# A hybrid decoder layer: ten of 22 row pairs of each down matrix in seven block products instead of eight, and a tile shared with the memory's keys and values

## The chip, the cores and the metric

The kernel runs on one core of one Trainium2 chip, as one program in one launch. The metric is the device time of one execution in microseconds (us), lower is better. In the text TensorE is PE, VectorE is DVE, ScalarE is ACT, GpSimd is POOL, and SyncE is SP, which issues every DMA.

## What is computed

One layer on 256 tokens of width 1024: a SwiGLU feed-forward with layer norm, three token mixers that share an input projection (window attention, block attention, and cross attention into 256 memory tokens), gates, an output projection with layer norm, and a second SwiGLU with layer norm. The change touches the two feed-forwards (hidden width 2816) and the place of the memory's keys and values.

```python
def swiglu(x, w_gate, w_up, w_down):
    return (jax.nn.silu(x @ w_gate) * (x @ w_up)) @ w_down

x = layer_norm(DN_ALPHA * x + 0.5 * swiglu(x, ffn1_w_gate, ffn1_w_up, ffn1_w_down), ln1_g, ln1_b)
...
kv = mem @ w_mem_kv + b_mem_kv
...
x = layer_norm(DN_ALPHA * x + 0.5 * swiglu(x, ffn2_w_gate, ffn2_w_up, ffn2_w_down), ln3_g, ln3_b)
```

## The kernel before

**Weights.** All weights lie in 1 MB chunks of 128 x 2048. A chunk is loaded into one of three raw buffers (tile `raw`), then split into a rounded part and a remainder: ACT casts `whi` (line 136), DVE subtracts and writes `wlo` (line 137). `whi` and `wlo` have four buffers each; a chunk's buffers come free when PE has made its last matmul with them. An fp32 product is three matmuls (`product`, lines 209 to 211): high by high, low by high, high by low. Near the end of the first feed-forward, from the last four chunks of its down matrix to the second feed-forward's chunk 3, a chunk is split in four quarters of 512 columns each.

**Feed-forward.** For each of 11 chunks of 256 hidden features, `ffn` makes the gate and up products, the activation, and the hidden tile `h`, split into `hh` and `hl`. Then `down` goes through the 11 chunks of the down matrix in the order of `DOWN[n]`; this text calls the place of a chunk in it its position, 0 to 10. An ordinary chunk makes eight products (2 rows of 128 features x 2 halves of the tokens x 2 halves of the columns), 24 matmuls of 512 columns. At the positions in `SEVEN` a chunk is taken as a 2 x 2 block product with seven multiplications (Strassen-Winograd), 21 matmuls. For this DVE makes four sums of `h` (lines 482 to 485), which are split like `h` into one of the tiles `pairs`, two chunks to a tile, and `seven_parts` (line 183) makes three sums of the weights into the one tile `t` (lines 188 to 190) and then splits three quarters of the raw chunk and `t` itself, so that it takes two `whi` and two `wlo` buffers.

```python
DOWN = {1: list(range(NC)), 2: [2, 0, 4, 1, 6, 3, 8, 5, 7, 9, 10]}
SEVEN = (0, 2, 4, 6)
KEEP = 3
```

The last three positions (`KEEP`) are held: their products are made for the first half of the tokens, then for the second, so that the norm of one half can begin while PE works on the other. Before them, after position 7, `settle` and `more` (lines 408 to 424) add the seven-product banks of PSUM into the residual `x_sb`: an ACT copy `e` of bank 1, then nine DVE instructions.

**After the first down stage.** `load_mem` (line 543) loads the 256 memory tokens transposed (tile `mem`, in the place of `t`) and splits them into `memT`, two tiles: one ACT cast and one DVE subtraction of 128 x 2048. PE goes on with the memory's keys (chunk `mk`, line 577), transposes of the normed tokens, the memory's values (`mv`), then the chunks `qa0`, `qa1` and `v0` of the input projection. Keys and values lie in `km` and `vm`, lines 560 and 561.

**The order.** SP's instructions run in the order in which the code writes them: `load_to` and `load_mem` in turn, so the load of the memory tokens is queued behind that of `qa0`'s chunk. The instructions of PE, ACT and DVE are put in order by a scheduler when the program is built; on the chip each engine runs its own in that order and waits on semaphores.

Of the kernel before, what the change touches and what calls it, by code (L numbers as in the profile page):

```python
# [11 lines left out]
F32R = mybir.dt.float32r  # L12
# [5 lines left out]
P = 128  # L18
S = 256
# [4 lines left out]
NC = NF // 2  # L24
# [5 lines left out]
SLOPES = [2.0 ** (-8.0 * (i + 1) / 6) for i in range(6)]  # L30


DOWN = {1: list(range(NC)), 2: [2, 0, 4, 1, 6, 3, 8, 5, 7, 9, 10]}
SEVEN = (0, 2, 4, 6)
KEEP = 3


# [3 lines left out]
def plan():  # L41
# [5 lines left out]
    def cols(name, c0):  # L47
        return lambda d: tiles(d[name][0][:, c0 : c0 + 256], 256)

    def rows(name, r0):  # L50
        return lambda d: tiles(d[name][0][r0 : r0 + 256], D)
# [11 lines left out]
    def half(name, i):  # L63

        return lambda d: tiles(d[name][0][i * 512 : (i + 1) * 512, :512], 512)
# [3 lines left out]
    def ffn(n):  # L69
        for c in range(NC):  # L70
            for k, w in (("g", "gate"), ("u", "up")):
                lead = n == 2 and c < 2
                chunks.append(((k, n, c), f"lead{k}" if lead and c == 0 else None,
                               half(f"ffn{n}_w_{w}", c) if lead else cols(f"ffn{n}_w_{w}", c * 256)))
        for i, c in enumerate(DOWN[n]):
            chunks.append((("d", n, c), "seven" if i in SEVEN else None, rows(f"ffn{n}_w_down", c * 256)))

# [43 lines left out]
def hybrid_layer(ctx: ExitStack, tc: tile.TileContext, a: dict, out: bass.AP):  # L121
# [4 lines left out]
    const = ctx.enter_context(tc.tile_pool(name="const", bufs=1))  # L126
    raws = ctx.enter_context(tc.tile_pool(name="raws", bufs=3))
    parts = ctx.enter_context(tc.tile_pool(name="parts", bufs=4))
    acts = ctx.enter_context(tc.tile_pool(name="acts", bufs=1))
# [4 lines left out]
    def split(src, hi, lo):  # L134

        nc.scalar.copy(hi, src)  # L136
        return nc.vector.tensor_sub(lo, src, hi.bitcast(F32))  # L137
# [58 lines left out]
    def weights(key, ahead=2):  # L196
        i = index[key]
        load_to(i + 6)
        part_to(i + ahead)
        return part_of.pop(i)  # L200
# [17 lines left out]
    def tok(t):  # L218
        return slice(t * P, (t + 1) * P)
# [5 lines left out]
    def feature_tile_2(ps, w, col, x, ks=range(KD), parts_=(0, 1)):  # L225

        for part in parts_:
            for k in ks:
                wk = w[part][:, k * 256 + col : k * 256 + col + P]
                if part == 0:  # L230
                    nc.tensor.matmul(ps, wk, x.both[:, k], start=k == 0, stop=False)  # L231
                else:
                    nc.tensor.matmul(ps[:, S:], wk, x[0][:, k], start=False, stop=k == KD - 1)  # L233

    def added(dst, ps):

        b = work.tile([P, 512], F32, name="b", tag="w")[:, :S]
        nc.scalar.copy(b, ps[:, S:])  # L238
        nc.vector.tensor_add(dst, ps[:, :S], b)
# [91 lines left out]
    def halves(name, tags):  # L331

        t = [acts.tile([P, n, S], F32R, name=f"{name}{i}", tag=tags[i]) for i, n in enumerate((12, 10))]
        return lambda k, n=1: t[0][:, k : k + n, :] if k < 12 else t[1][:, k - 12 : k - 12 + n, :]
# [37 lines left out]
    def down(n, lhs, sums, resid, after, between=None, ends=HALVES):  # L372


        order = DOWN[n]
        bank = {b: acc.tile([P, 512], F32, name="ps") for b in (1, 6, 5, 7, 2, 3, "x", 4)}
        n7, n8 = len(SEVEN), len(order) - KEEP - len(SEVEN)
        left = {b: n7 for b in (1, 5, 6, 7)} | {b: n7 + 2 * (n8 + KEEP) for b in (2, 3, 4)} | {"x": 2 * n8}
# [13 lines left out]
        for i, c in enumerate(order):  # L392
            w = weights(("d", n, c), 1 if i >= len(order) - KEEP else 2)
            if i in SEVEN:
                (s1, s2, s3, s4), (b, t) = sums[c], w
# [44 lines left out]
    def gated(g, u):  # L440

        s = work.tile([P, 512], F32, name="s", tag="w")
        nc.scalar.activation(s, g, AF.Silu)
        h = work.tile([P, 512], F32, name="h", tag="w")
        nc.vector.scalar_tensor_tensor(h, u, 0.5, s, op0=ALU.mult, op1=ALU.mult)
        return h

    def ffn(n, x, resid, after, start=0, hooks={}, h=None, between=None, ends=HALVES):
        hh, hl = h or (halves("hh", ("A1", "A2")), halves("hl", ("B1", "B2")))
        sevens = [DOWN[n][i] for i in SEVEN]  # L450
        pairs = [acts.tile([P, 2, 2, 4, P], F32R, name=f"s{i}", tag=t) for i, t in enumerate(("C", "E"))]
        sums = {}
        for c in range(start, NC):
            if c in hooks:
                hooks[c](hh, hl)
            gu = []

            ps = {}
            for ks in FIRST if n == 1 and c == 0 else [range(KD)]:
                for key in ("g", "u"):  # L460
                    if ks.start == 0:
                        ps[key] = weights((key, n, c)), [mm.tile([P, 512], F32, name="ps") for _ in range(2)]
                    if len(ks) < KD:
                        for part in range(2):
                            for j in range(2):
                                feature_tile_2(ps[key][1][j], ps[key][0], j * P, x, ks, (part,))
                    else:
                        for j in range(2):
                            feature_tile_2(ps[key][1][j], ps[key][0], j * P, x)
                    if ks.stop == KD:  # L470
                        v = work.tile([P, 512], F32, name=key, tag="w")
                        for j in range(2):
                            added(v[:, j * S : (j + 1) * S], ps[key][1][j])
                        gu.append(v)
            y = gated(*gu)
            split(y.rearrange("p (j s) -> p j s", s=S), hh(2 * c, 2), hl(2 * c, 2))
            if c in sevens:

                a11, a21, a12, a22 = (y[:, tok(i)] for i in range(4))
                s = work.tile([P, 512], F32, name="s", tag="w")  # L480
                s1, s2, s3, s4 = (s[:, tok(i)] for i in range(4))
                nc.vector.tensor_add(s1, a21, a22)
                nc.vector.tensor_sub(s3, a11, a21)
                nc.vector.tensor_sub(s2, s1, a11)
                nc.vector.tensor_sub(s4, a12, s2)
                i = sevens.index(c)
                both = pairs[i // 2][:, i % 2]
                split(s.rearrange("p (i c) -> p i c", c=P), both[:, 0], both[:, 1])
                sums[c] = [(both[:, 0, m], both[:, 1, m]) for m in range(4)]
        down(n, lambda k, t: (hh(k)[:, 0, tok(t)], hl(k)[:, 0, tok(t)]), sums, resid, after, between, ends)  # L490
# [59 lines left out]
    def norm1(t, pss):  # L550
        if "x1" not in late:
            late["x1"] = const.tile([P, 2, D], F32, name="x1_sb", tag="X1")
        norm_into(x_sb, late["x1"], scale=1.0)(t, pss)

    ffn(1, x0T, x_sb, norm1, hooks={4: hook_1, 7: hook_2}, between=load_mem)
    memT, x1 = late["memT"], late["x1"]
    x1T = tokens_of("x1T")


    km = tuple(const.tile([P, 2, S], F32R, name=f"km{i}") for i in range(2))  # L560
    vm = tuple(const.tile([P, 2, 256], F32R, name=f"vm{i}") for i in range(2))

    def biased(ps, bc, hi, lo):

# [265 lines left out]
    def finish(t, pss):  # L830
        def put(t, s, r):
            return r, lambda: nc.sync.dma_start(out=out[0, tok(t), s], in_=r)
        normalize(t, pss, x2, put, scale=1.0)

    ffn(2, x2T, x2, finish, start=2, hooks={3: hook_lead}, h=h2, ends=((0, 512), (512, 768), (768, D)))
    for key in ("g", "u"):
        queue_behind(x2T_last, lows[index[key, 2, 2]])
# [30 lines left out]
```

## Time and profile before

| | us |
|---|---|
| median of 3 runs | 573.85 |
| lowest and highest | 573.81, 574.36 |
| the profiled execution | 573.77 |
| its span, first to last instruction | 572.0 |
| PE busy in the span | 561.8 (98%) |
| DVE busy | 452.7 (79%) |
| ACT busy | 326.2 (57%) |

The profile is of one execution. The span leaves out 1.77 us of the profiled execution's time that lies around it. A busy PE is an engine with an instruction under way; where two matmuls follow each other at the pace of their width, it does not wait. Idle time of DVE or ACT costs nothing by itself.

### The profile page before, as it was taken

To read this page: it belongs to the slowest core of one execution; us is meant where nothing else is said; L and a number is where in the kernel's file an instruction comes from. 1 tells how busy PE (TensorE), PEld (TensorE's weight loads), DVE (VectorE), ACT (ScalarE), POOL (GpSimd) and SP (SyncE) were. 2 spreads that over 40 slices of the span, in tenths; PEclk is the share of its full clock that TensorE was granted. 3 is DMA by queue.
4 is the path that set the end of the run, shared out by engine and by line. 5 is a ranking of instruction groups with operands and counts; after the bars stand their busy time and mean duration, and the time that the engine had idled before them with its cause. 6 is when DMAs were issued, how large, how long until landed. Compare 5 with 4: busy or idle time off the path is not lost.

```text
span 572.0 us, 8735 instructions
## 1 busy us (share of the span) xinstructions
PE 561.8 (98%) x3378; PEld 498.3 (87%) x3378; DVE 452.7 (79%) x707; ACT 326.2 (57%) x569; POOL 23.6 (4%) x37
## 2 busy tenths in 40 slices
PE   8999999999999999999999999999999999999994
PEld 7888888888888998999999999888888888888883
DVE  5898667878888998699787677997666777889686
ACT  6786555546653652965974765543565656464600
POOL 2000000000000000000002022210000000000001
PEclk9999999999999999999999999999999999999998
DMA  8886756535655275084163655546555645444502
GB/s 277 311 296 260 282 172 269 178 119 213 227 222 221 80 298 211 7 347 164 29 226 116 220 170 200 183 156 248 222 182 187 201 167 210 158 149 170 199 0 73
DMA packets 18025, 108.98 MB, mean 191 GB/s; under 512 B 2112, under 2 KB 2368, under 8 KB 5696
## 3 DMA queue, kind: packets, MB, share of 16 engines
q1 hardware_dynamic: 17984, 108.43, 52.5%
q8 instruction: 26, 0.43, 0.3%
q14 instruction: 15, 0.12, 0.1%
HBM read 107.37 MB, written 1.05 MB: 190 GB/s over the span
## 4 chain that ended last, share of the span: by engine, by line
PE 92%; ACT 3%; DVE 2%; DMA 1%; issue 0%; SPq 0%; POOLq 0%; DVEq 0%
PE ps L231 29%; PE ps L210 15%; PE ps L209 15%; PE ps L211 15%; PE ps L233 15%; ACT whi L136 1%; DMA xT<-in_xT_dram 1%; ACT sc_b L664 1%; PE ps L688 1%; PE ps L277 1%; DVE sc_b L648 1%; DVE m L653 0%; PE ps L641 0%; ACT gates L724 0%; DVE r L523 0%
## 5 line engine op out<-in xcount | busy, mean ns | idle before, releaser
L137 DVE TENSOR_TENSOR wlo<-raw,whi 128x512 fp32r<-128x512 f32 (+3 forms) x242 | 230.2, 983 | 64.1 <-ACT whi L136 57.7
L136 ACT CAST whi<-raw 128x512 fp32r<-128x512 f32 (+3 forms) x242 | 194.0, 845 | 96.8 <-PE ps L211 39.7
L231 PE MATMUL ps<-x0T,whi 128*128 128x512 f32 x352 | 89.5, 393 | 0.9 <-DVE x0T L137 0.5
L231 PEld LDWEIGHTS ps<-x0T,whi 128*128 128x128 f32 x352 | 62.8, 189 | 12.2 <-ACT whi L136 1.3
L231 PE MATMUL ps<-x2T,whi 128*128 128x512 f32 x288 | 72.2, 392 | 0.0
L231 PEld LDWEIGHTS ps<-x2T,whi 128*128 128x128 f32 x288 | 51.8, 189 | 9.3
L209 PE MATMUL ps<-x1T,whi 128*128 128x256 f32 x192 | 55.2, 287 | 0.3 <-ACT sc_m L664 0.3
L211 PE MATMUL ps<-x1T,wlo 128*128 128x256 f32 x192 | 54.3, 283 | 0.0
L210 PE MATMUL ps<-x1T,whi 128*128 128x256 f32 x192 | 54.3, 283 | 0.0
L210 PE MATMUL ps<-wlo,hh 128*128 128x512 f32 (+1 forms) x142 | 54.0, 380 | 0.0
L209 PE MATMUL ps<-whi,hh 128*128 128x512 f32 (+1 forms) x142 | 54.0, 380 | 0.0
L211 PE MATMUL ps<-whi,hl 128*128 128x512 f32 (+1 forms) x142 | 54.0, 380 | 0.0
L233 PEld LDWEIGHTS ps<-x0T,wlo 128*128 128x128 f32 x352 | 48.8, 190 | 4.1 <-DVE wlo L137 0.2
L233 PE MATMUL ps<-x0T,wlo 128*128 128x256 f32 x352 | 50.0, 282 | 0.0
L238 ACT COPY b<-ps 128x256 f32<-128x256 f32 x92 | 33.4, 368 | 25.8 <-PE ps L233 24.2
L233 PEld LDWEIGHTS ps<-x2T,wlo 128*128 128x128 f32 x288 | 39.3, 190 | 2.8
L233 PE MATMUL ps<-x2T,wlo 128*128 128x256 f32 x288 | 40.2, 282 | 0.0
L209 PEld LDWEIGHTS ps<-x1T,whi 128*128 128x128 f32 x192 | 36.8, 191 | 0.8 <-ACT sc_m L664 0.5
L210 PEld LDWEIGHTS ps<-x1T,whi 128*128 128x128 f32 x192 | 36.8, 192 | 0.0
L211 PEld LDWEIGHTS ps<-x1T,wlo 128*128 128x128 f32 x192 | 36.8, 191 | 0.0
L209 PEld LDWEIGHTS ps<-whi,hh 128*128 128x128 f32 x142 | 26.7, 188 | 5.1
L210 PEld LDWEIGHTS ps<-wlo,hh 128*128 128x128 f32 x142 | 26.7, 188 | 5.1
(195 smaller groups left out, 892.9 us busy)
## 6 DMA issues: line engine op xcount, KB each, us to landing
raw<-in_w_dram SPq DMA_DIRECT2D x92, 1024.0 KB, 4.8
raw<-in_w_dram SPq DMA_DIRECT2D x16, 256.0 KB, 5.3
ln<-in_ln_dram SPq DMA_DIRECT2D x3, 1024.0 KB, 7.0
xT<-in_xT_dram SPq DMA_DIRECT2D x4, 256.0 KB, 6.3
x_sb<-in_x_dram SPq DMA_DIRECT2D x1, 1024.0 KB, 7.0
mem<-in_memT_dram SPq DMA_DIRECT2D x1, 1024.0 KB, 8.4
out_dram<-r SPq DMA_DIRECT2D x3, 256.0 KB, 2.0
brow<-in_by_column_dram SPq DMA_DIRECT2D x1, 387.0 KB, 8.4
```

The costliest lines, as they stand in the source:

```text
L136: nc.scalar.copy(hi, src)
L137: return nc.vector.tensor_sub(lo, src, hi.bitcast(F32))
L209: nc.tensor.matmul(ps, lh, rh, start=first and i == 0, stop=False)
L210: nc.tensor.matmul(ps, lh, rl, start=False, stop=False)
L211: nc.tensor.matmul(ps, ll, rh, start=False, stop=last and i == n - 1)
L231: nc.tensor.matmul(ps, wk, x.both[:, k], start=k == 0, stop=False)
L233: nc.tensor.matmul(ps[:, S:], wk, x[0][:, k], start=False, stop=k == KD - 1)
L238: nc.scalar.copy(b, ps[:, S:])
L277: nc.tensor.transpose(ps[:, j * P : (j + 1) * P], src[:, k * P : (k + 1) * P], ident)
L648: nc.vector.scalar_tensor_tensor(sc[:, len(raw), :], dist[nm], -SLOPES[h] / SCALE, ps[:, :w], op0=ALU.mult, op1=ALU.add)
L664: nc.scalar.activation(sc[:, e, c0:c1], raw[e][:, c0:c1], AF.Exp, bias=negm[:, e, t : t + 1], scale=SCALE, accum_out=ssum[:, e, t : t + 1])
L688: nc.tensor.transpose(pt[:, s * n + j * P : s * n + (j + 1) * P], sc[:, 2 * i + s, c : c + P], ident)
```

## The change

`SEVEN` gets a fifth position and is now 0, 1, 3, 5 and 7, for both feed-forwards; `DOWN[2]` is put in another order, so that the chunks computed first come first. The block sums of the fifth chunk need a third tile. It is a tile of the constant pool under the name `KV`, and the memory's keys and values, which were four tiles of their own, are now slices of one tile `kv` of the same size in the same place: the sums of the first feed-forward lie there before the keys and values are written, those of the second after they were last read.

```diff
-DOWN = {1: list(range(NC)), 2: [2, 0, 4, 1, 6, 3, 8, 5, 7, 9, 10]}
-SEVEN = (0, 2, 4, 6)
+DOWN = {1: list(range(NC)), 2: [2, 3, 0, 4, 1, 6, 5, 8, 7, 9, 10]}
+SEVEN = (0, 1, 3, 5, 7)
...
-        pairs = [acts.tile([P, 2, 2, 4, P], F32R, name=f"s{i}", tag=t) for i, t in enumerate(("C", "E"))]
+        pairs = [pool.tile([P, 2, 2, 4, P], F32R, name=f"s{i}", tag=t)
+                 for i, (pool, t) in enumerate(((acts, "C"), (acts, "E"), (const, "KV")))]
...
-    km = tuple(const.tile([P, 2, S], F32R, name=f"km{i}") for i in range(2))
-    vm = tuple(const.tile([P, 2, 256], F32R, name=f"vm{i}") for i in range(2))
+    kv = const.tile([P, 4, 2, S], F32R, name="kv", tag="KV")
+    km, vm = (tuple(kv[:, 2 * j + i] for i in range(2)) for j in range(2))
```

Over both feed-forwards PE has 30 matmuls of 512 columns fewer with `hh` and `hl` and 24 more with the sums, six fewer in all. SP's and POOL's instructions stand as before. The scheduler put those of DVE, ACT and PE in another order around the down stages. (Line numbers from `ffn` on are one higher in the changed kernel.)

DVE in the middle of the first down stage, one position of eight products and the next of seven. Before, from the remainder of position 4's `t` (1477) over positions 5 (1512) and 6 (1542 its chunk, 1545 its sums `t`) to the remainder of position 6's `t` (1544):

```order
L137 TENSOR_TENSOR wlo_1477<-t_1478,whi_1476 128x2048
L188 TENSOR_TENSOR t_1545<-raw_1405 128x1024
L137 TENSOR_TENSOR wlo_1512<-raw_1344,whi_1511 128x2048
L189 TENSOR_TENSOR t_1545<-raw_1405,t_1545 128x512
L190 TENSOR_TENSOR t_1545<-raw_1405,t_1545 128x512
L137 TENSOR_TENSOR wlo_1542<-raw_1405,whi_1541 128x512
L137 TENSOR_TENSOR wlo_1542<-raw_1405,whi_1541 128x1024
L137 TENSOR_TENSOR wlo_1544<-t_1545,whi_1543 128x2048
```

In the changed kernel, from the remainder of position 3's `t` (1455) over positions 4 (1490) and 5 (1520, 1523) to the remainder of position 5's `t` (1522):

```order
L137 TENSOR_TENSOR wlo_1455<-t_1456,whi_1454 128x2048
L137 TENSOR_TENSOR wlo_1490<-raw_1295,whi_1489 128x2048
L188 TENSOR_TENSOR t_1523<-raw_1352 128x1024
L137 TENSOR_TENSOR wlo_1520<-raw_1352,whi_1519 128x512
L189 TENSOR_TENSOR t_1523<-raw_1352,t_1523 128x512
L137 TENSOR_TENSOR wlo_1520<-raw_1352,whi_1519 128x1024
L190 TENSOR_TENSOR t_1523<-raw_1352,t_1523 128x512
L137 TENSOR_TENSOR wlo_1522<-t_1523,whi_1521 128x2048
```

The three sums into `t` stood ahead of the chunk's own remainders; now they alternate with them, and the last sum (line 190) stands directly ahead of the remainder of `t`.

ACT at the end of the first down stage, from the copy `e` of bank 1: `whi` of position 10, of `mk`, of `mv`, `qa0` and `qa1`, in quarters. Before (1707 is position 10, 1719 `mk`, 1844 `mv`, 1924 `qa0`, 2012 `qa1`):

```order
L418 COPY e_1681<-ps_1397 128x512
L136 CAST whi_1707<-raw_1539 128x512 x4
L136 CAST whi_1719<-raw_1576 128x512 x4
L136 CAST whi_1844<-raw_1612 128x512 x2
L136 CAST memT0_1699<-mem_1697 128x2048
L136 CAST whi_1844<-raw_1612 128x512 x2
L136 CAST whi_1924<-raw_1645 128x512 x4
```

In the changed kernel (1716 is position 10, 1728 `mk`, 1850 `mv`, 1930 `qa0`, 2018 `qa1`):

```order
L418 COPY e_1690<-ps_1415 128x512
L136 CAST whi_1716<-raw_1554 128x512 x4
L136 CAST whi_1728<-raw_1584 128x512 x4
L136 CAST whi_1850<-raw_1621 128x512 x4
L136 CAST whi_1930<-raw_1657 128x512 x3
L136 CAST memT0_1708<-mem_1706 128x2048
L136 CAST whi_1930<-raw_1657 128x512
```

The cast of the memory tokens stood behind two quarters of `mv`; now it stands behind all four of `mv` and three of `qa0`.

PE among the held positions, first half of the tokens (1401 and 1402 are the two banks of its columns; 1647 and 1707 positions 9 and 10). Before:

```order
L210 MATMUL ps_1401<-wlo_1648,hh1_192 128x512
L211 MATMUL ps_1401<-whi_1647,hl1_194 128x512
L209 MATMUL ps_1401<-whi_1707,hh1_192 128x512
L210 MATMUL ps_1401<-wlo_1708,hh1_192 128x512
L211 MATMUL ps_1401<-whi_1707,hl1_194 128x512
```

In the changed kernel (1419 and 1420 the two banks, 1422 a bank of the second half; 1623, 1659 and 1716 positions 8, 9 and 10):

```order
L210 MATMUL ps_1420<-wlo_1717,hh1_192 128x512
L211 MATMUL ps_1420<-whi_1716,hl1_194 128x512
L210 MATMUL ps_1419<-wlo_1717,hh1_192 128x512
L211 MATMUL ps_1419<-whi_1716,hl1_194 128x512
L209 MATMUL ps_1420<-whi_1716,hh1_192 128x512
L209 MATMUL ps_1422<-whi_1623,hh1_192 128x512
L210 MATMUL ps_1422<-wlo_1624,hh1_192 128x512
L210 MATMUL ps_1420<-wlo_1717,hh1_192 128x512
```

Before, position 10's products of one bank followed each other; now its products with the later quarters of `wlo_1717` are put off behind products of the other bank and of the second half of the tokens.

## Rows read from the trace of the kernel before

**Rows 1.** Top of the page, parts 1 and 2.
```profile
span 572.0 us, 8735 instructions
...
PE 561.8 (98%) x3378; PEld 498.3 (87%) x3378; DVE 452.7 (79%) x707; ACT 326.2 (57%) x569; POOL 23.6 (4%) x37
...
PEclk9999999999999999999999999999999999999998
```

**Rows 2.** Waits of the weight loads: total us, times, longest.
```profile
PEld ps L209 <- ACT sc_m L664: 0.5, 1, 0.5
PEld ps L210 <- DVE memT L137: 0.2, 1, 0.2
PEld ps L210 <- DVE p L137: 0.5, 2, 0.3
```

**Rows 3.** TensorE timeline: start us, duration us, instruction.
```profile
129.84 0.40 PE L209 MATMUL ps<-whi,hh 128*128 128x512 f32 x1
...
140.07 0.39 PE L209 MATMUL ps<-whi,hh 128*128 128x512 f32 x1
...
170.67 0.39 PE L209 MATMUL ps<-whi,hh 128*128 128x512 f32 x1
...
186.99 0.40 PE L209 MATMUL ps<-memT,whi 128*128 128x256 f32 x2
187.42 0.39 PE L210 MATMUL ps<-memT,whi 128*128 128x256 f32 x1
...
506.49 0.40 PE L209 MATMUL ps<-whi,hh 128*128 128x512 f32 x1
...
563.78 0.28 PE L211 MATMUL ps<-whi,hl 128*128 128x256 f32 x1
```

**Rows 4.** VectorE timeline, the two down stages; columns as above.
```profile
144.30 2.29 DVE L137 TENSOR_TENSOR wlo<-t,whi 128x2048 fp32r<-128x2048 f32 x1 [0.94 <-ACT whi L136]
146.63 1.23 DVE L188 TENSOR_TENSOR t<-raw 128x1024 f32<-128x1024 f32 x1
147.77 2.28 DVE L137 TENSOR_TENSOR wlo<-raw,whi 128x2048 fp32r<-128x2048 f32 x1
149.97 0.68 DVE L189 TENSOR_TENSOR t<-raw,t 128x512 f32<-128x512 f32 x1
150.69 0.69 DVE L190 TENSOR_TENSOR t<-raw,t 128x512 f32<-128x512 f32 x1
...
156.71 2.49 DVE L137 TENSOR_TENSOR wlo<-raw,whi 128x512 fp32r<-128x512 f32 x4
...
166.19 0.68 DVE L414 SCALAR_TENSOR_TENSOR x_sb<-x_sb,e 128x512 f32<-128x512 f32 x1
166.79 0.68 DVE L410 TENSOR_TENSOR y<-e,ps 128x512 f32<-128x512 f32 x1
...
173.40 3.09 DVE L137 TENSOR_TENSOR wlo<-raw,whi 128x512 fp32r<-128x512 f32 x5
...
520.95 2.29 DVE L137 TENSOR_TENSOR wlo<-t,whi 128x2048 fp32r<-128x2048 f32 x1 [0.94 <-ACT whi L136]
```

**Rows 5.** Busy us by engine in 160 to 180, clock.
```profile
160.00:180.00 20.00, 20.00 (x90) 16.55 (x89) 17.34 (x29) 9.09 (x17) 0.00 (x0) 1.00 0.67 248
```

**Rows 6.** ScalarE timeline, end of the first down stage.
```profile
129.09 1.57 ACT L136 CAST whi<-raw 128x512 fp32r<-128x512 f32 x2 [1.41 <-PE ps L231]
...
181.75 1.14 ACT L136 CAST whi<-raw 128x512 fp32r<-128x512 f32 x2 [8.70 <-PE ps L211]
182.95 1.91 ACT L136 CAST memT<-mem 128x2048 fp32r<-128x2048 f32 x1
```

**Rows 7.** SyncE timeline, issue of the memory load.
```profile
174.48 0.43 SPq L546 DMA_DIRECT2D mem<-in_memT_dram  x1
```

**Rows 8.** Memory tile's own view, time from issue to landing.
```profile
DMA to landing us min/median/max: 8.4/8.4/8.4
```

**Rows 9.** Engines and granted clock of the last stretch, columns as rows 5.
```profile
568.00:570.00 2.00, 0.00 (x0) 0.00 (x0) 0.50 (x2) 0.00 (x0) 0.00 (x0) 0.53 0.74 262
```

## The prediction

> **What bounds the kernel now.** The top of the page first: PE is busy in 561.8 of 572.0 us, at the full clock [rows 1]. Then the waits: those of the weight loads show how little PE waits for, 0.2 to 0.5 us here and there, one of them for the remainder of the memory tokens [rows 2]. Then PE's timeline in the first down stage. Positions 0 and 1 take 140.07 - 129.84 = 10.23 us for 21 + 24 = 45 matmuls, so one of 512 columns takes 0.227 us, a seven-product position 4.77 us and an eight-product one 5.44 us [rows 3]. No gap is left there, so a matmul less is 0.227 us less, as long as DVE and ACT deliver. DVE is the next engine: 17.3 of 20 us in the second half of that stage [rows 5]. The last view is what stands at the end of that stage. PE reaches the memory's keys at 186.99 and starts its first matmul with the remainder of `memT` at 187.42 [rows 3], where two of 256 columns ahead of it (0.12 us each, by the page's pace of 512) would have let it start at about 187.23: that is the 0.2 us of the wait. This place is already on the edge.
>
> **What is removed.** In each feed-forward one position goes from 24 matmuls to 21: 3 x 0.227 = 0.68 us, both 1.36 us, all on PE's path.
>
> **What is added.** The fifth chunk's sums of `h` and its longer split are DVE and ACT work beside PE. I replay the changed order with durations of before, first stage first. Up to 129.84 I take PE as unmoved: the gate and up products are the same, and the extra sums of `h` (under 2 us of DVE a chunk by the rows of 128 to 512 columns) fall where no weight wait is seen.
>
> Steps on DVE, from one start to the next: 2048 columns 2.20, 1024 columns 1.14, 512 columns 0.60 [rows 4]; the cast of 2048 on ACT 1.91 [rows 6]. Hand-over between the two engines: 0.03 us, an estimate.
>
> Position 1 is now a seven right behind another, and the cast of its `t` needs the `whi` buffer of the last up chunk, free at 129.09 [rows 6]. It ends at 131.00, its remainder runs 131.03 to 133.3; PE needs it ten matmuls into position 1, at 136.9. Then come in order an addition of 256 columns (0.34, an estimate from its half width), line 188, `h`, position 2's remainder, `hl`, line 189, a quarter, a quarter's worth of line 190 to its end (0.69), with the rest of position 3's chunk filling the cast: 133.23 + 0.34 + 1.14 + 0.60 + 2.20 + 0.60 + 0.60 + 0.60 + 0.69 = 140.00; the cast of position 3's `t` starts only now and its remainder at 141.98.
>
> From here each pair of an eight and a seven costs DVE: remainder of `t` 2.20, remainder of the eight 2.20, line 188 1.14, a quarter 0.60, line 189 0.60, half a chunk 1.14, line 190 to its end 0.69, then the bare cast 1.98 = 10.55 us. Before, the three sums stood earlier and the cast lay beside other DVE work, so only 0.94 us of a wait remained [rows 4]. PE's pair takes 10.21 us. So DVE loses 0.34 us a pair, but from a lead: the remainders of `t` of positions 3, 5 and 7 start at 141.98, 152.53 and 163.08 and end by 144.3, 154.8 and 165.4, and PE needs them at 146.9, 157.1 and 167.5. No wait of PE so far.
>
> **The end of the first stage.** Before, the splits of positions 7, 8 and 9 are twelve quarters and the settling starts at 166.19 [rows 4]. Now DVE is free of position 7 at 165.28; eight quarters (2.41 for four, as 156.71's row less its overlap) bring it to 170.10, where the settling starts, 3.9 us later. Bank 6, which the second settling instruction reads, is complete 18 matmuls into position 7, at 169.5, in time. The four quarters of position 10 follow at the distances of before, the last starting 173.40 - 166.19 = 7.21 after the first settling instruction: 177.31, ending 177.99. PE starts the held positions at 170.67 - 0.68 = 169.99 and, in its new order, needs the third and the fourth quarter of the remainder as its 32nd and 37th matmul, at 177.02 and 178.15; they are there at 176.8 and 178.0. So no wait, by 0.2 us; had the order been that of before, the third would have been wanted at 174.97. PE ends the stage at 186.99 - 0.68 = 186.31.
>
> **The new wait.** Two things now hold the memory tokens. First the load: SP issues it right behind `qa0`'s chunk, whose raw buffer is free when position 10's last quarter is split. Before, the last quarter (started 173.40) ended at 174.0 and the load was issued at 174.48 [rows 4, 7]; now 177.99 + 0.48 = 178.47, and with 8.4 us to landing [rows 8] it is there at 186.9. Second ACT: the cast stands behind three quarters of `qa0`, which need the `whi` buffer of position 9. PE reads that until six matmuls before the end of the stage; with the release of before (position 8's last matmul starts 181.33, the cast 181.75 [rows 6]) it is free at 185.14, and three casts (1.14 for two, so 1.66) reach 186.8. Both causes give the same time, so mending one alone would not help. Cast 186.9 to 188.85, remainder 188.88 to 191.16, PE's first matmul with it at 191.2, against 187.42: **3.8 us later**, the 0.68 us already in it. PE makes two matmuls in between and stands about 4.5 us. Before, the cast ran at 182.95, in time.
>
> Behind this, DVE has 13.9 us of work from the start of that remainder to the last remainder of the turned tokens, which PE needs 15.4 us after it (2.3 + the 13.1 us from 187.42 to the first product with them, both sums counted along the two timelines): covered, by about 0.5 us after its waits for PE. If that cover goes, it costs those tenths. The scores, gates and projections behind keep their order; the few waits left there [rows 2] may shrink, since DVE and ACT have more time: at most the 1.0 us that the first and the third row hold, at least nothing. I take nothing.
>
> **The second feed-forward.** Its down stage repeats the first, shifted by 506.49 - 129.84 = 376.65 on PE and 520.95 - 144.30 = 376.65 on DVE [rows 3, 4], and the changed order repeats too. Position 10 is split in one piece here, at 547.5 to 549.8, ahead of most of the settling; PE needs it at 174.29 + 376.65 = 550.9. No load and no next product stand behind. The 0.68 us is kept to the end.
>
> **The shared tile** moves no instruction of PE and adds none; its sums and the keys are tens of us apart on both sides. Nothing, bounded by the least of the waits shown, 0.2 us either way.
>
> **The sum.** Span 572.0 + 3.8 - 0.7 = 575.1, and 1.77 around it: 576.9 against the profiled 573.77. The median stands 0.08 above that: **577.0 us**, 0.55% slower. 0.2% of the time, 1.15 us, is about what a measurement of this kernel can tell from no change.
>
> **The rivals.** *Faster: the cover holds.* The memory tokens' cast would have to start by 182.0, so that its remainder is there at 186.3. For it: PE has no other wait in the sum. Against it: both the load and the buffer would have to be 5 us earlier than replayed. It gives 573.85 - 1.36 = 572.5. Chance 0.07.
>
> *A shorter wait.* DVE holds its lead better than replayed and `qa0`'s casts find a free buffer, so that the cast starts at 184 to 185 and the loss is under 1.1 us: 573.0 to 575.0. Against it: the buffer's release is PE's own. Chance 0.08.
>
> *DVE is later than replayed.* A lead of 0.2 us at position 10 is within the error of some thirty steps added up. Each 0.5 us that DVE is later moves the load and makes PE wait for a quarter as well: up to 578.2 for 1.2 us. This is the upper part of the forecast's own range, not another case; its lower end is 575.8, with the later waits gone. Forecast's chance 0.77.
>
> *The clock falls in the wait.* After the last matmul (563.78) the granted clock was still 1.00 up to 568, then 0.53 in the mean of 568 to 570, so half speed after some 4 us of rest [rows 3, 9]; the new rest is 4.5 us, broken by two matmuls. At 1.2 GHz each of the 46 matmuls left of the keys takes about 0.12 us more: a third of them 1.8 us, all 5.5. That gives 578.8 to 582.5. Against it: the two matmuls in between. Chance 0.08.
>
> The Trainium skill ("TensorE: Matmul & The Clock Gate", Part 1) says that the array's clock is throttled by default and that activity releases it; the row of 568 to 570 agrees, and no row here shows a rest with two matmuls in it.
>
> **How the numbers follow.** Slower is the forecast and the clock, 0.85; the same 0.08; faster 0.07. The range leaves out those two cases and most of the clock's, 0.20: from 575.6, a little under the forecast's lower end, to 579.2, which takes in the cheapest of the clock's.
>
> **What would show it.** Right: PE's matmuls of 512 columns fall by six; DVE's settling starts near 170; SP's load of the memory tokens near 178.5; the cast of `memT` near 187 and PE's first matmul with its remainder near 191; a wait of PE on it of about 4 us; the second down stage 0.7 us shorter. Wrong: that wait under 1 us, or a wait of PE on a remainder `wlo` before the end of the stage, or a clock under 1.00 near 190.

## The result: 0.9% slower, 5.0 us

| | before | changed |
|---|---|---|
| median, lowest and highest of 6 runs (us) | 573.83 (573.46 to 574.36) | 578.86 (578.45 to 582.06) |
| ratio, 95% interval | | 1.0094 (1.0084 to 1.0105) |
| profiled execution, its span (us) | 573.77, 572.0 | 579.02, 577.2 |
| mean granted clock of that execution | 0.997 | 0.989 |

The direction was forecast. The median lies at the upper end of the range of 575.6 to 579.2; the ratio, which is a little above that of the medians (1.0088), gives 1.0094 x 573.85 = 579.24, just outside it. The likeliest case, 577.0, is 1.9 us short of the median. The change cost 5.0 us where 3.15 were forecast.

The page of the changed kernel, parts 1 and 2, as [rows 1] of before:

```profile
span 577.2 us, 8742 instructions
...
PE 563.3 (98%) x3372; PEld 499.2 (86%) x3372; DVE 460.9 (80%) x724; ACT 329.0 (57%) x572; POOL 23.6 (4%) x37
...
PEclk9999999999999799999999999999999999999998
```

The six matmuls are gone (3378 to 3372), and one slice of 40 has a clock of 0.7. TensorE's timeline there (start, duration, instruction), the end of the first down stage, the products with the memory tokens, and the transposes behind them; it answers to [rows 3]:

```profile
186.36 0.39 PE L211 MATMUL ps<-whi,hl 128*128 128x512 f32 x1
188.94 0.58 PE L209 MATMUL ps<-memT,whi 128*128 128x256 f32 x2 [2.19 <-ACT memT L136]
191.27 0.58 PE L210 MATMUL ps<-memT,whi 128*128 128x256 f32 x1 [1.75 <-DVE memT L137]
...
198.97 0.49 PE L277 MATMUL ps<-ident,x_sb 128*128 128x128 f32 x3
```

Before, the transposes stood here:

```profile
193.04 1.04 PE L277 MATMUL ps<-ident,x_sb 128*128 128x128 f32 x8
```

The wait for the memory tokens is there, in two pieces, and the first matmul with their remainder is at 191.27, forecast at 191.2. From 187.42 that is 3.85 us. But the transposes, 5.62 us behind that matmul before (193.04), are 7.70 us behind it now: 2.08 us more, for the same 46 matmuls. The windows of that stretch (busy time and number of instructions of PE, its weight loads, DVE, ACT and POOL, then the granted clock, the share of the DMA engines, GB/s) show why:

```profile
187.00:188.00 1.00, 0.00 (x0) 0.00 (x0) 1.00 (x3) 1.00 (x2) 0.00 (x0) 1.00 0.38 156
188.00:189.00 1.00, 0.06 (x1) 0.06 (x1) 0.77 (x3) 1.00 (x2) 0.00 (x0) 1.00 0.04 16
189.00:190.00 1.00, 0.52 (x2) 0.24 (x2) 1.00 (x1) 1.00 (x3) 0.00 (x0) 0.61 0.30 49
190.00:191.00 1.00, 0.00 (x0) 0.00 (x0) 1.00 (x1) 1.00 (x3) 0.00 (x0) 0.50 0.68 254
...
195.00:196.00 1.00, 1.00 (x7) 1.00 (x6) 1.00 (x3) 0.00 (x0) 0.00 (x0) 0.50 0.00 0
196.00:198.00 2.00, 2.00 (x18) 2.00 (x18) 1.59 (x4) 0.48 (x1) 0.00 (x0) 0.99 0.00 0
```

The same in shorter windows, around the fall:

```profile
189.00:189.20 0.20, 0.20 (x2) 0.20 (x2) 0.20 (x1) 0.20 (x1) 0.00 (x0) 1.00 0.00 0
189.20:189.40 0.20, 0.20 (x2) 0.04 (x1) 0.20 (x1) 0.20 (x2) 0.00 (x0) 0.54 0.00 0
```

The clock falls to half (1.2 GHz) at 189.2, inside the wait, and stays there until 196, while TensorE is busy again from 191.27: 5 matmuls of 256 columns start between 195 and 196, 8 between 197 and 198, at full clock. At half clock 22 of the 46 start, 0.21 us apart instead of 0.12. From the transposes to the second down stage nothing more is lost or gained on balance: that stage starts at 512.41, 5.92 us late, and ends 5.24 us late, 0.68 us back. The span's account is 3.85 + 2.08 - 0.01 - 0.68 = 5.24. It is the account of one execution: the six took 578.45 to 582.06 us at mean granted clocks of 0.994 to 0.987, and only that of 579.02 has a trace.

What holds the memory tokens, that is, what keeps their cast from starting, is as replayed. VectorE: the remainders of `t` of positions 3, 5 and 7 and the first settling instruction; ScalarE: the quarters of `mv` and `qa0` and the cast; SyncE: the load (start, duration, instruction, idle time ahead of it):

```profile
142.08 2.29 DVE L137 TENSOR_TENSOR wlo<-t,whi 128x2048 fp32r<-128x2048 f32 x1 [0.90 <-ACT whi L136]
...
152.71 2.29 DVE L137 TENSOR_TENSOR wlo<-t,whi 128x2048 fp32r<-128x2048 f32 x1 [2.05 <-ACT whi L136]
...
163.33 2.29 DVE L137 TENSOR_TENSOR wlo<-t,whi 128x2048 fp32r<-128x2048 f32 x1 [2.05 <-ACT whi L136]
...
170.35 0.69 DVE L414 SCALAR_TENSOR_TENSOR x_sb<-x_sb,e 128x512 f32<-128x512 f32 x1
```

```profile
181.35 2.18 ACT L136 CAST whi<-raw 128x512 fp32r<-128x512 f32 x4 [6.25 <-PE ps L211]
185.43 1.66 ACT L136 CAST whi<-raw 128x512 fp32r<-128x512 f32 x3 [1.90 <-PE ps L211]
187.00 1.89 ACT L136 CAST memT<-mem 128x2048 fp32r<-128x2048 f32 x1
```

```profile
178.65 0.43 SPq L547 DMA_DIRECT2D mem<-in_memT_dram  x1
```

```profile
DMA to landing us min/median/max: 8.1/8.1/8.1
```

Before, DVE waited 0.94 us for the cast of position 4's `t`, and the cast of the tokens ran at 182.95 [rows 4, 6]. Now the load lands at 178.65 + 8.1 = 186.75, and the three quarters of `qa0` end at 187.1.

### The profile page after: what moved, and what is told of

Read it like the earlier page. It is cut to its first block, busy times and chain, and to the rows that moved or that the text cites. A ratio compares the mean times of both kernels' runs of the same rounds, so it can differ in the third digit from the quotient of the medians.

```text
span 577.2 us, 8742 instructions
## 1 busy us (share of the span) xinstructions
PE 563.3 (98%) x3372; PEld 499.2 (86%) x3372; DVE 460.9 (80%) x724; ACT 329.0 (57%) x572; POOL 23.6 (4%) x37
## 4 chain that ended last, share of the span: by engine, by line
PE 91%; ACT 4%; DVE 2%; DMA 1%; issue 0%; SPq 0%; POOLq 0%; DVEq 0%
PE ps L231 29%; PE ps L210 15%; PE ps L209 15%; PE ps L233 15%; PE ps L211 15%; ACT whi L136 2%; DMA xT<-in_xT_dram 1%; ACT sc_b L665 1%; PE ps L689 1%; PE ps L277 1%; DVE sc_b L649 1%; DVE m L654 0%; DVE memT L137 0%; PE ps L642 0%; ACT gates L725 0%
## 5 line engine op out<-in xcount | busy, mean ns | idle before, releaser
L210 PE MATMUL ps<-wlo,hh 128*128 128x512 f32 (+1 forms) x132 | 50.2, 381 | 0.0
L211 PE MATMUL ps<-whi,hl 128*128 128x512 f32 (+1 forms) x132 | 50.0, 380 | 0.0
L209 PE MATMUL ps<-whi,hh 128*128 128x512 f32 (+1 forms) x132 | 49.8, 380 | 0.0
L137 DVE TENSOR_TENSOR wlo<-t,whi 128x2048 fp32r<-128x2048 f32 x10 | 22.9, 2293 | 20.3 <-ACT whi L136 20.3
L136 ACT CAST whi<-t 128x2048 fp32r<-128x2048 f32 x10 | 19.1, 1910 | 29.2 <-DVE t L190 23.5
```

What stands on the lines that cost most here:

```text
L209: nc.tensor.matmul(ps, lh, rh, start=first and i == 0, stop=False)
L210: nc.tensor.matmul(ps, lh, rl, start=False, stop=False)
L211: nc.tensor.matmul(ps, ll, rh, start=False, stop=last and i == n - 1)
```

## Experiments

All times are medians; ratios are to the kernel before on the same chip, 573.9 us in each comparison.

**1. The clock by itself.** TensorE is kept busy in the wait, with no change on the other engines.

```diff
         ps = mm.tile([P, 512], F32, name="ps")
+        if j == 0:
+            for _ in range(72):
+                nc.tensor.matmul(ps[:, :P], idle, idle, start=True, stop=True)
         feature_tile(ps[:, :S], w, j * P, memT)
```

> The changed kernel with 72 small products of zeros (128 columns each, into the bank of the memory's keys, which their own first product overwrites) put on TensorE between the end of the first down stage and the first matmul with the memory tokens. ACT, DVE and SP keep their order. Theory (the loss is a wait of 3.85 us for the memory tokens, and 2.1 us more because the granted clock falls to half in that wait): the remainder of memT is still first read at about 191.3, the granted clock stays at 1.00 from 187 to 198, and the 2.1 us come back: 576.8 us. Rival (the 2.1 us behind the wait are DVE and ACT work that has become late, and the low clock only goes with it): no change, 578.9 us.

577.26 us (576.55 to 577.85), ratio 1.0057 (1.0044 to 1.0069). TensorE, then the windows:

```profile
186.83 4.19 PE L580 MATMUL ps<-idle 128*128 128x128 bf16 x72
190.83 0.36 PE L209 MATMUL ps<-memT,whi 128*128 128x256 f32 x1
191.50 0.38 PE L210 MATMUL ps<-memT,whi 128*128 128x256 f32 x1 [0.31 <-DVE memT L137]
```

```profile
187.00:189.00 2.00, 2.00 (x39) 2.00 (x37) 1.90 (x4) 2.00 (x2) 0.00 (x0) 1.00 0.33 135
189.00:191.00 2.00, 2.00 (x38) 1.99 (x35) 1.84 (x1) 1.76 (x5) 0.00 (x0) 1.00 0.45 94
191.00:193.00 2.00, 1.69 (x14) 1.50 (x13) 2.00 (x4) 1.07 (x3) 0.00 (x0) 1.00 1.02 430
193.00:196.00 3.00, 3.00 (x27) 3.00 (x26) 3.00 (x7) 0.47 (x1) 0.99 (x1) 1.00 0.03 8
```

The remainder is read at the same place (191.50; this execution began its first down stage 0.22 us later), the clock stays at 1.00, and the transposes start 1.73 us sooner (197.24), 1.95 against the stage's start. DVE and ACT kept their order, so the rival falls: the 2 us are the clock's. In the medians 1.6 came back, not 2.1 (by the ratios, 1.0094 to 1.0057, it is 2.1); the profiled execution lost 0.46 us again around 398.8, in short waits at the second feed-forward's first chunk, which the changed kernel's profile does not have. The Trainium skill ("TensorE: Matmul & The Clock Gate", Part 1) says that activity releases the throttle of the array; these windows agree: with TensorE busy on products of zeros the granted clock stayed at 1.00.

**2. Each hold alone.** First the load ahead of `qa0`'s, with the cast held where it was; then the cast ahead of `qa0`'s quarters, with the load where it was.

```diff
# load alone (between() now only loads; the split is behind the stage)
             w = weights(("d", n, c), 1 if i >= len(order) - KEEP else 2)
+            if i == 6 and between:
+                between()
...
-                if between:
-                    between()
...
+    prepare("qa0")
+    split_mem()
+    queue_behind(highs[index["qa0"]][2], [late["cast"]])
+    queue_behind(late["cast"], highs[index["qa0"]][3:])
+    queue_behind(late["last"], lows[index["qa0"]])
...
# cast alone
     w = weights("mk", 1)
+    prepare("qa0")
+    queue_behind(late["cast"], highs[index["qa0"]])
```

> The changed kernel with the load of the memory tokens ahead of qa0's as in the run before, but with their cast held where the changed kernel has it, behind three quarters of qa0 on ACT. Theory (two holds that end at the same time, 186.8 by the load and 187.0 by the quarters' buffer): the cast still starts near 187.0, the clock falls again: 578.9 us, within 0.5. Rival (the late load is the cause): the cast starts well before 187 and most of the 5 us come back, 572.5 to 575 us.

> The changed kernel with the memory tokens' cast put ahead of qa0's quarters on ACT, and their load left where the changed kernel has it, behind qa0's. Theory (two holds that end at the same time): the cast waits for the load, which lands at about 186.8, so it starts within 0.3 us of 187.0, the clock falls again: 578.6 us. Rival (the cast's place on ACT alone is the cause): the cast starts well before 187, 572.5 to 575 us.

Load alone: 579.46 us (578.33 to 580.65), ratio 1.0095 (1.0081 to 1.0109). Cast alone: 579.21 us (578.03 to 579.46), ratio 1.0089 (1.0076 to 1.0102). ScalarE with the load alone, and its load's time to landing (issued at 171.1):

```profile
185.71 1.66 ACT L138 CAST whi<-raw 128x512 fp32r<-128x512 f32 x3 [1.89 <-PE ps L214]
187.28 1.89 ACT L138 CAST memT<-mem 128x2048 fp32r<-128x2048 f32 x1
```

```profile
DMA to landing us min/median/max: 7.1/7.1/7.1
```

ScalarE with the cast alone:

```profile
187.22 1.90 ACT L138 CAST memT<-mem 128x2048 fp32r<-128x2048 f32 x1 [3.43 <-DMA mem<-in_memT_dram]
```

With the load alone the tokens lay there from 178.2 and the cast still ran at 187.28, behind the quarters. With the cast alone ScalarE stood idle for 3.43 us and started it at 187.22, when the load had landed. Either hold is enough for the loss, and mending one gains nothing.

**3. Both holds away.** The load as above, and the split behind the stage without the forced place; the scheduler then puts the cast directly behind `mk`'s quarters.

> The changed kernel with both holds on the memory tokens taken away: their load is issued ahead of qa0's instead of behind it (at position 6, behind mv's), and their cast then stands ahead of the quarters of mv and qa0 on ACT, their remainder ahead of them on DVE. Theory: TensorE does not wait for them and the clock holds; both stages keep their three matmuls: 573.85 - 1.36 = 572.5 us, faster than the kernel before. Rival (DVE in the first down stage is full, and the 2.3 us of the remainder, now inside it, make another wait there): 573.5 to 576 us, with a wait of TensorE on a wlo or on the norm of the first half.

573.52 us (572.92 to 573.82), ratio 0.9990 (0.9981 to 0.9999). The wait and the fall of the clock are gone: 5.3 us. The rest of the theory was 1.0 us too good. TensorE and ScalarE show a new wait, for `v0`'s first quarter:

```profile
201.35 0.50 PE L209 MATMUL ps<-whi,x1T 128*128 128x512 f32 x1 [0.68 <-ACT whi L136]
```

```profile
200.68 0.62 ACT L136 CAST whi<-raw 128x512 fp32r<-128x512 f32 x1 [2.73 <-DMA raw<-in_w_dram]
```

The last quarter of `mv`'s remainder was on DVE at 195.11, behind the memory tokens' remainder and the norm of both halves, and only then was the raw buffer for `v0` free. The rival had the mechanism (no room on DVE), though not the place. A further run puts that quarter ahead of the second half's norm.

```diff
-                nc.vector.scalar_tensor_tensor(r, r, mv[:, 0:1], ln_g[:, s], op0=ALU.subtract, op1=ALU.mult)
+                centred = nc.vector.scalar_tensor_tensor(r, r, mv[:, 0:1], ln_g[:, s], op0=ALU.subtract, op1=ALU.mult)
+                late.setdefault(("centred", t), centred)
...
     w = weights("mk", 1)
+    queue_behind(lows[index["mv"]][-1], [late["centred", 1]])
```

> The run with both holds taken away (573.52 us), and the last quarter of mv's remainder put on DVE ahead of the norm of the second half of the tokens. That run kept a wait of 0.84 us at 201.3: TensorE waits for v0's chunk, whose load was issued at 195.8, when mv's last quarter had freed its raw buffer. Theory: the load is issued 1.5 us or more earlier, the wait goes and nothing else does: 573.52 - 0.84 = 572.7 us. Rival (DVE has no time to give there: the norm of the second half, 0.6 us later, makes TensorE wait for its transposes instead): 573.3 us or more.

572.99 us (572.46 to 573.45), ratio 0.9984 (0.9975 to 0.9992). The quarter starts at 192.90, the cast of `v0` at 198.55; TensorE's stalls there, the one of 0.84 us and 0.10 just behind it, shrink to about 0.55 in all and not to nothing. The larger part of what is left is a wait for a remainder of the turned tokens, which VectorE makes at 200.22: that is the rival's mechanism. In the medians 0.53 us came back of the 0.84 expected.

**4. The order on DVE.** The three sums of the weights stand ahead of the chunk's remainders again.

```diff
-        nc.vector.tensor_sub(t[:, 1536:], raw[:, 1024:1536], t[:, 1024:1536])
-        for o in (slice(0, 512), slice(1024, 2048)):
-            split(raw[:, o], bh[:, o], bl[:, o])
+        last = nc.vector.tensor_sub(t[:, 1536:], raw[:, 1024:1536], t[:, 1024:1536])
+        queue_behind(last, [split(raw[:, o], bh[:, o], bl[:, o]) for o in (slice(0, 512), slice(1024, 2048))])
```

> The changed kernel with the three sums of the weights put ahead of the chunk's own remainders on DVE again, as the kernel before had them, so that ACT's cast of t runs beside those remainders; loads and all else as in the changed kernel. Theory (the new order leaves the cast bare, 1.1 to 2.05 us a pair, and that is what makes DVE 4.2 us later at the settling and with it the load of the memory tokens): settling near 167.5, load issued near 175.5, the remainder of memT there near 188.5, a wait of TensorE of about 2 us in two pieces, no fall of the clock: 574.0 us, 573 to 575. Rival (it is the amount of DVE's work, not its order): settling still near 170, 578.9 us.

574.67 us (574.02 to 578.58), ratio 1.0028 (1.0015 to 1.0041). VectorE, then TensorE:

```profile
150.96 2.29 DVE L137 TENSOR_TENSOR wlo<-t,whi 128x2048 fp32r<-128x2048 f32 x1 [0.32 <-ACT whi L136]
...
160.09 2.29 DVE L137 TENSOR_TENSOR wlo<-t,whi 128x2048 fp32r<-128x2048 f32 x1 [0.32 <-ACT whi L136]
...
168.80 0.68 DVE L413 SCALAR_TENSOR_TENSOR x_sb<-x_sb,e 128x512 f32<-128x512 f32 x1
```

```profile
186.56 0.48 PE L208 MATMUL ps<-memT,whi 128*128 128x256 f32 x2
188.87 0.39 PE L209 MATMUL ps<-memT,whi 128*128 128x256 f32 x1 [1.83 <-DVE memT L137]
```

The windows behind that wait, columns as above:

```profile
188.00:189.00 1.00, 0.13 (x1) 0.13 (x2) 1.00 (x2) 1.00 (x4) 0.00 (x0) 1.00 0.00 0
189.00:190.00 1.00, 1.00 (x9) 1.00 (x10) 1.00 (x3) 1.00 (x3) 0.00 (x0) 1.00 0.00 0
```

A pair costs DVE 160.09 - 150.96 = 9.13 us instead of 163.33 - 152.71 = 10.62, because the wait for the cast of `t` falls from 2.05 to 0.32. The tokens' load is issued at 176.49, their cast runs at 184.58, and TensorE stands idle 1.83 us instead of 2.19 + 1.75 = 3.94. In this profile the clock does not fall. The same kernel's longer executions (575.6 to 578.6) have a mean granted clock of 0.990 to 0.993, the shorter ones (574.0 to 574.7) 0.995 to 0.998, which points to a fall of the clock in some executions and not in others; those longer ones have no trace. The settling came at 168.80, not near 167.5: ahead of it DVE waits 1.59 us for ScalarE's quarters. Counted from the start of the down stage in each profile, the order gave back 1.8 of the 4.1 us by which the settling had become late, and 2.4 of 4.1 at the issue of the load. So the order is about half of DVE's lateness; what the rest is, this run does not separate.

The last version takes this order together with the run at 572.99.

> The run at 572.99 us (both holds away, mv's last quarter early) together with the sums of the weights ahead of the chunk's remainders on DVE, as the kernel before had them. Theory: the wait of 0.10 us at 177.4 for position 10's remainder goes, and DVE's lead of 1.5 us carries over to mv's quarters, so that the 0.43 us at 200.5 go too: 572.5 us, 0.24% under the kernel before. Rival (behind 181 DVE waits for TensorE's own results, so its lead is lost there): 572.9 us.

572.18 us (571.63 to 572.41), ratio 0.9967 (0.9954 to 0.9979), the fastest of all. Its tokens' remainder starts at 180.69 on DVE, and TensorE goes from the down stage into the keys without a gap:

```profile
185.62 0.39 PE L210 MATMUL ps<-whi,hl 128*128 128x512 f32 x1
185.85 0.28 PE L208 MATMUL ps<-memT,whi 128*128 128x256 f32 x1
185.96 0.28 PE L209 MATMUL ps<-memT,whi 128*128 128x256 f32 x1
```

The waits at 177.4 and 200.5 are gone too. That the median is 0.3 us better than expected is not explained; the profiled execution began its first down stage 0.46 us sooner than that of before, and such starts range from 129.54 to 130.17 over the three runs here that keep the order of before up to it (experiments 5 and 6).

**5. The same place without the change.** The kernel before, with the tokens' cast moved on ScalarE, and the remainders of `qa0` put behind theirs on VectorE.

```diff
# in the kernel before
+    prepare("qa0")
+    split_mem()
+    queue_behind(highs[index["qa0"]][2], [late["cast"]])
+    queue_behind(late["cast"], highs[index["qa0"]][3:])
+    queue_behind(late["last"], lows[index["qa0"]])
...
```

> The kernel before, four positions of seven products in each stage, with only the memory tokens' cast moved: on ACT it stands behind mv's four quarters and three of qa0, as in the changed kernel, and their remainder behind it on DVE. Theory (the place of the cast alone makes the loss, whatever the products): qa0's quarters wait for position 9's buffer until 185.8, the cast runs at 187.4, the remainder is there at 191.6, 4.2 us later than before, and the clock falls to half for some 7 us, 2.1 us more: 580.2 us. Rival (the fall of the clock, or part of the wait, needs the fuller DVE of the changed kernel): 578.1 us or less, with a granted clock of 1.00 behind the wait.

581.24 us (580.05 to 581.51), ratio 1.0127 (1.0112 to 1.0143). ScalarE, VectorE, TensorE and the windows:

```profile
187.10 1.89 ACT L138 CAST memT<-mem 128x2048 fp32r<-128x2048 f32 x1
```

```profile
189.98 2.29 DVE L139 TENSOR_TENSOR memT<-mem,memT 128x2048 fp32r<-128x2048 f32 x1
```

```profile
189.05 0.50 PE L212 MATMUL ps<-memT,whi 128*128 128x256 f32 x2 [2.19 <-ACT memT L138]
192.32 0.58 PE L213 MATMUL ps<-memT,whi 128*128 128x256 f32 x1 [2.77 <-DVE memT L139]
```

```profile
191.00:192.00 1.00, 0.00 (x0) 0.00 (x0) 1.00 (x1) 0.59 (x2) 0.00 (x0) 1.00 0.00 0
192.00:193.00 1.00, 0.68 (x3) 0.68 (x4) 1.00 (x3) 0.00 (x0) 0.00 (x0) 0.54 0.00 0
193.00:194.00 1.00, 1.00 (x7) 1.00 (x7) 1.00 (x2) 0.00 (x0) 0.00 (x0) 0.50 0.00 0
```

Four positions, no added work, a load that is there at 182.5, and the whole loss: the cast's place is enough to make it. The remainder ran 0.7 us later than I had put it, since DVE had the second half's norm in hand, and TensorE read it at 192.32, 4.90 us later than before. The clock fell again, here only just behind 192, and was back at about 195.5; the 46 matmuls took 7.01 us, 1.39 more than before. 4.90 + 1.39 = 6.29 is what this execution lost (580.05 against 573.77); the other three took 1.1 to 1.5 us longer and have no trace. The two matmuls in between, at 189.05, had ended some 2.5 us before the clock fell here, while in the changed kernel it fell with them under way.

**6. The second feed-forward and the tile alone.**

```diff
-SEVEN = (0, 1, 3, 5, 7)
+SEVEN = {1: (0, 2, 4, 6), 2: (0, 1, 3, 5, 7)}
# tile alone: both (0, 2, 4, 6), DOWN[2] of before
```

> Five positions of seven products in the second feed-forward alone; the first has the four and the order of before; keys and values share the tile. Theory: the second stage gains its three matmuls and nothing else moves: 573.85 - 0.68 = 573.2 us. Rival (the shared tile, or the new order in the second stage, costs something too): 573.8 us or more.

> The four positions and the order of before in both feed-forwards; only the memory's keys and values are slices of one tile. Theory: no instruction moves and nothing waits: 573.85 us, within 0.4. Rival (one tile makes writes and reads of keys and values wait for each other): 574.3 us or more, with a wait on kv.

Second alone: 573.25 us (572.64 to 573.58), ratio 0.9987 (0.9978 to 0.9996); a gain of 0.7 us as expected. Tile alone: 573.72 us (573.28 to 574.16), ratio 0.9997 (0.9988 to 1.0006), no difference. In its profile TensorE's waits from the first down stage on are those of before, with 0.19 us at 187.7 for the tokens' remainder. So of the changed kernel's parts the second stage gains what its matmuls take, the tile costs nothing, and the loss is all in the first.

## Why the prediction was right and wrong

| step | forecast (us) | measured |
|---|---|---|
| remainders of `t`, positions 3, 5, 7 | 141.98, 152.53, 163.08 | 142.08, 152.71, 163.33 |
| DVE a pair | 10.55 | 10.63, 10.62 |
| settling starts | 170.1 | 170.35 |
| the stage ends | 186.31 | 186.59 (its last matmul starts at 186.36, 0.23 each) |
| memory tokens: load issued, there | 178.47, 186.9 | 178.65, 186.75 |
| cast, remainder begins, read | 186.9, 188.88, 191.2 | 187.00, 188.92, 191.27 |
| wait to the remainder, net | 3.8 | 3.85 |
| second stage | 0.68 back | 0.68 back |
| clock | 1.00; if it falls, 1.8 to 5.5 | falls; 2.08 |

**Right.** The place, the two holds that end together, the size of the wait and the gain of the second stage. Experiments 2 and 3 show both holds, and that mending one alone does not help, as the prediction said. The tile cost nothing (experiment 6). No wait followed at the turned tokens, also in experiment 1, where the clock did not fall and TensorE reached them without that delay.

**Wrong: the clock.** The sum put nothing for the clock. The step that failed is the reason for that, the argument against the fourth rival, "the two matmuls in between": they start at 188.94, and the clock is at 0.54 of full speed in the window of 189.2 to 189.4. The runs showed 2.08 us in its place. A clock under 1.00 near 190 and a wait on a `wlo` before the end of the stage were both on the prediction's own list of what would show it wrong. I had counted the rest as 4.5 us broken by two matmuls, had one row of a rest at the end of the span [rows 9], and gave the fall 0.08. Its price at the low end, 1.8 us for a third of the matmuls, came close to the 2.08 measured, in part by luck: 22 of the 46 ran at half clock, nearly half and not a third, and each cost 0.09 us more, not 0.12. The 578.8 forecast for the case against a median of 578.86 is as lucky, since the executions spread to 582.06. It should have shared the weight with the forecast at the least: the one row of a rest spoke for the fall, and against it stood no row. Experiment 1 shows the clock as the cause of that part, experiment 5 that a like rest takes it down in the kernel before as well. Where in the rest it falls, and so what it costs, differed between the two traces (2.08 and 1.39 us); why is open.

**A little wrong: the quarters of position 10.** "No wait, by 0.2 us" was a wait of 0.10 us at 177.43. The replay was 0.25 us early by then: 0.10 at the first of the three remainders and 0.07 to 0.08 in each pair behind it.

**The faster rival.** 572.5 us needed the tokens 5 us sooner. With both holds away (experiment 3) the same seven-product positions give 573.0 and, with the order on DVE of before, 572.2. Against the kernel before on the same chip, 573.96, the last is 1.8 us faster, more than the 1.36 that the saved matmuls were costed at. The 0.19 us of the old wait for the tokens is in it; the rest is not explained, and the first stage's 0.68 us was not measured by itself.

## What to carry to other kernels

Count for every engine what the new order puts ahead of the first work behind a stage, its loads too, because a cast that the scheduler moves a few places can cost more than the change saves. When two holds end at the same time, find both before mending either. A wait of TensorE may cost more than its own length: here 3.9 us of idle time brought 2.08 us at half clock behind it, and products of zeros in the wait took that away. So cost the stretch at half clock as a case of its own, with weight.

## What was not expected of the hardware

- The granted clock did not come back with TensorE's work: it was at 0.50 from 189.4 to 196.0, though TensorE was busy again from 191.27. The half-speed stretch behind the wait cost 2.08 us, about half as much as the wait.
- It fell while the two matmuls between the two pieces of the wait were under way, after an idle stretch of 2.19 us (in experiment 5 after two, of 2.19 and 2.77 us).
- With 1.83 us of idle time in the traced execution (experiment 4) the mean granted clock differed between executions of one kernel, 0.990 to 0.998, and the times with it, 574.0 to 578.6.
